# First projection rows of a two-layer decoder kernel: columns for shift and scale, sigmoid by the exponential, new planner costs

## The chip, the cores and the metric

The program runs on one core of one Trainium2 chip. The metric is the device time of one execution in microseconds; the median of three runs of the kernel before is 709.39 us. A core has five engines that run their own instruction streams and meet through semaphores: PE (TensorE, the matrix multiplier), DVE (VectorE), ACT (ScalarE), POOL (GpSimd) and SP (SyncE, which here only issues the DMA transfers). 16 DMA engines move data between HBM and SBUF.

## The reference, cut to what matters

Two layers over x of 256 rows and 1024 columns, all in float32. Each layer first makes six vectors of 1024 from the conditioning vector c, and uses two of them, shift and scale, on the normalized rows before its projections:

```python
cond = jax.nn.silu(c)                                  # c * sigmoid(c), 1024 numbers
for l in range(DEPTH):
    mod = (cond @ w_mod[l] + b_mod[l])[:, None, :]     # w_mod[l]: 1024 x 6144
    sh_a, sc_a, g_a, sh_f, sc_f, g_f = jnp.split(mod, N_MOD, axis=-1)
    h = rms_norm(x, norm_mix[l]) * (1 + sc_a) + sh_a
    proj = h @ w_in[l]                                 # 1024 x 3072: mq mk mv dq dk dv
    ...
    x = x + g_a * (jnp.concatenate([o_m, o_d], axis=-1) @ w_out[l])
    h = rms_norm(x, norm_ffn[l]) * (1 + sc_f) + sh_f
    x = x + g_f * ((jax.nn.silu(h @ w_gate[l]) * (h @ w_up[l])) @ w_down[l])
```

The weights are read once from HBM, some 157 MB. Only for layer 0 is nothing computed yet when its shift and scale are needed; for everything later they can be prepared beside other work.

## The kernel before, in words

**Products.** Every large product is made of float32 operands split in two parts, hi and lo, that TensorE multiplies at its faster float32 rate: `mm3` (L466 to L478) issues three matmuls of 128 x 512, hi*hi (L473), lo*hi (L474) and hi*lo (L475). There are 784 such triples in a fixed chain, in the order of the program text; the kernel's progress can be counted in them. `split` makes the two parts of a weight tile: ACT copies (`hi`, L463), DVE subtracts (`lo`, L464). Other matmuls (attention, transposes, the modulation) are plain float32.

**A planner sets the order.** The kernel text doesn't emit instructions but records them (`op`), and a list scheduler (`Plan.schedule`) puts them in order per engine, from a cost of each operation, latencies between engines (`DRAIN`, `WAKE`, `DMA_DONE`), the cost of a DMA (`c_dma`) and a rank for each group of operations (the table `RANK`, `TUNE`). Its times are used for the order alone. At run time each engine goes through its list strictly in that order and waits where an operand isn't there. All DMAs stand in one list on SP. Buffers are few: 3 of 1 MiB (`raw`), 2 of 512 KiB (`rawm`), 8 pairs of `hi` and `lo`, 12 of 256 KiB (`w`), 8 banks of PSUM (`ps`); a transfer waits until its buffer's last reader is done.

**The start of layer 0** (`start_layer0`) is the part that the change rewrites. It loads x, takes 1/rms of its rows (`x_rstd`, L552 squares on ACT), and goes through five blocks of output columns, of 1, 1, 2, 2 and 2 times 128 (`blocks`). For each block it needs the shift and the scale of these columns. w_mod comes in pieces in which partition p holds rows 8p to 8p+7, so that one block is eight terms (t = 0..7), each a 128-row product with one column of `cs` (silu(c)). The first `npe[b]` terms are matmuls (L923) of a stationary tile `cb`, in which each `cs` column is repeated 128 times, with w_mod as the moving operand: the result is the row, repeated on all partitions. The other terms are accumulated on DVE (`acc`, L926) and summed over partitions by one more matmul with ones (L928). Then: the scale row plus one times the gain row (L933, the gain loaded to all partitions), the shift row copied (L935, ACT), for both row tiles of x the scaling (L938) and the shift (L941), transposes on PE (L943), and the split of the transposed result into `hThi` (L949, ACT) and `hTlo` (L951, DVE). With these, and with the split rows of w_in for the same columns k, PE runs 6 triples for each of the 8 k (dq, dk and dv for two row tiles): 48 triples, after which the dq, dk and dv of layer 0 are complete.

```python
op(ACT, 1400.0, lambda: S.activation(cs.tile, cs.tile, AF.Silu), [cs], [cs])
```

This line (L448) makes silu(c) with a table of ACT that has to be loaded for it, and again a load for the tables used later (L449).

**Beside this** DVE accumulates the other sections of w_mod for the two layers (`mod_section`, L513: 80 instructions of 128 x 1024).

Of the kernel before, what the change touches and what calls it, by code (L numbers as in the profile page):

```python
# [52 lines left out]
class Op:  # L53
    __slots__ = ("eng", "cost", "fn", "deps", "succ", "left", "bufs", "tail", "boost", "idx", "ready", "end", "start", "soft", "main", "group")


class Plan:
# [1136 lines left out]
```

## Time and profile before

| | us |
|---|---|
| median of 3 runs | 709.39 |
| lowest, highest | 708.60, 710.76 |
| the profiled execution | 709.06 |
| its span, from the first to the last instruction | 706.9 |
| PE busy in the span | 666.8 (94%) |
| DVE busy | 528.5 (75%) |
| ACT busy | 391.2 (55%) |
| DMA queue of the loads, share of the 16 engines | 65.4% |

Times inside the trace are counted from the first instruction. A float32 matmul that isn't a transpose stands in the trace as two records, so L923 with 13 instructions has 26. Matmul records overlap, since they are pipelined: what one costs in a row of many is the distance from one start to the next, not its duration. The order of an engine's list tells what stands behind what, and only the trace tells how long.

### The profile page before, as it was taken

To read this page: it belongs to the slowest core of one execution; us is meant where nothing else is said; L and a number is where in the kernel's file an instruction comes from. 1 tells how busy PE (TensorE), PEld (TensorE's weight loads), DVE (VectorE), ACT (ScalarE), POOL (GpSimd) and SP (SyncE) were. 2 spreads that over 40 slices of the span, in tenths; PEclk is the share of its full clock that TensorE was granted. 3 is DMA by queue.
4 is the path that set the end of the run, shared out by engine and by line. 5 is a ranking of instruction groups with operands and counts; after the bars stand their busy time and mean duration, and the time that the engine had idled before them with its cause. 6 is when DMAs were issued, how large, how long until landed. Compare 5 with 4: busy or idle time off the path is not lost.

```text
span 706.9 us, 8834 instructions
## 1 busy us (share of the span) xinstructions
PE 666.8 (94%) x3085; PEld 520.7 (74%) x3085; DVE 528.5 (75%) x846; ACT 391.2 (55%) x836; POOL 17.0 (2%) x37
## 2 busy tenths in 40 slices
PE   2988999997999999999989999999999999999997
PEld 1656767775778887878768886788788888888885
DVE  3979899999886778787778998996886554464433
ACT  5335899755454544453345766998755444544420
POOL 2000020000000000000000000000000000000000
PEclk9999999999899999999999999999999999999999
DMA  8988885656678679888883589453537555555501
GB/s 267 346 279 296 314 304 178 219 168 227 221 252 284 230 264 313 304 315 295 268 290 134 192 295 318 175 190 110 179 119 249 188 187 194 194 179 178 179 1 59
DMA packets 92496, 158.25 MB, mean 224 GB/s; under 512 B 6030, under 2 KB 62234, under 8 KB 92452
## 3 DMA queue, kind: packets, MB, share of 16 engines
q1 hardware_dynamic: 92452, 157.69, 65.4%
q8 instruction: 24, 0.39, 0.2%
q14 instruction: 20, 0.16, 0.1%
HBM read 156.62 MB, written 1.05 MB: 223 GB/s over the span
## 4 chain that ended last, share of the span: by engine, by line
PE 56%; DMA 14%; issue 12%; DVE 11%; ACT 4%; SPq 1%; POOL 1%; DVEq 0%; ACTq 0%; POOLq 0%
PE ps L475 16%; PE ps L473 16%; PE ps L474 16%; DMA rawm<-in_w_mod_dram 7%; DVE acc L513 4%; DVE lo L464 3%; DMA raw<-in_w_mod_dram 3%; DMA raw<-in_w_in_dram 2%; ACT hi L463 2%; PE ps L674 2%; PE ps L923 1%; PE ps L735 1%; PE ps L1079 1%; ACT w L609 1%; DMA raw<-in_w_down_dram 1%
## 5 line engine op out<-in xcount | busy, mean ns | idle before, releaser
L464 DVE TENSOR_TENSOR lo<-raw,hi 128x1024 fp32r<-128x1024 f32 (+1 forms) x192 | 230.6, 1210 | 99.7 <-ACT hi L463 99.2
L463 ACT ACTIVATE hi<-raw 128x1024 fp32r<-128x1024 f32 (+1 forms) x192 | 198.9, 1050 | 170.8 <-PE ps L475 119.1
L473 PE MATMUL ps<-hi,hThi 128*128 128x512 f32 x544 | 224.0, 412 | 1.9 <-ACT w L609 1.3
L475 PE MATMUL ps<-hi,hTlo 128*128 128x512 f32 x544 | 216.8, 398 | 0.0
L474 PE MATMUL ps<-lo,hThi 128*128 128x512 f32 x544 | 216.5, 398 | 0.0
L473 PEld LDWEIGHTS ps<-hi,hThi 128*128 128x128 f32 x544 | 103.5, 190 | 27.2 <-issue 1.4
L475 PEld LDWEIGHTS ps<-hi,hTlo 128*128 128x128 f32 x544 | 103.0, 189 | 25.6 <-DVE hTlo L951 0.7
L474 PEld LDWEIGHTS ps<-lo,hThi 128*128 128x128 f32 x544 | 103.5, 190 | 24.9 <-issue 1.4
L513 DVE SCALAR_TENSOR_TENSOR acc<-rawm,cs,acc 128x1024 f32<-128x1024 f32 x80 | 102.5, 1281 | 21.5 <-DMA rawm<-in_w_mod_dram 18.7
L473 PE MATMUL ps<-hi,oThi 128*128 128x512 f32 x240 | 96.7, 403 | 3.1 <-ACT oThi L1086 2.3
L474 PE MATMUL ps<-lo,oThi 128*128 128x512 f32 x240 | 95.7, 399 | 1.6 <-DVE lo L464 1.6
L475 PE MATMUL ps<-hi,oTlo 128*128 128x512 f32 x240 | 95.8, 399 | 1.0 <-DVE oTlo L1088 0.8
L473 PEld LDWEIGHTS ps<-hi,oThi 128*128 128x128 f32 x240 | 45.4, 189 | 13.9 <-ACT oThi L1086 2.8
L474 PEld LDWEIGHTS ps<-lo,oThi 128*128 128x128 f32 x240 | 45.4, 189 | 13.4 <-DVE lo L464 3.2
L475 PEld LDWEIGHTS ps<-hi,oTlo 128*128 128x128 f32 x240 | 45.3, 189 | 12.7 <-DVE oTlo L1088 1.2
L692 ACT ACTIVATE w<-ps,sm,sm 128x128 f32<-128x128 f32 (+1 forms) x64 | 32.6, 530 | 7.0 <-DVE sm L687 7.0
L1077 ACT ACTIVATE w<-ps 128x256 f32<-128x256 f32 x44 | 16.7, 382 | 24.0 <-PE ps L475 23.8
L923 PE MATMUL ps<-raw,w 128*128 128x512 f32 (+1 forms) x26 | 14.4, 690 | 14.8 <-DMA raw<-in_w_mod_dram 14.8
L1078 DVE TENSOR_TENSOR w<-w,ps 128x256 f32<-128x256 f32 x44 | 18.1, 416 | 6.1 <-ACT w L1077 6.1
L552 ACT ACTIVATE w<-xs 128x512 f32<-128x512 f32 x16 | 10.0, 627 | 20.9 <-DVE xs L782 19.1
L926 DVE SCALAR_TENSOR_TENSOR acc<-raw,cs,acc 128x512 f32<-128x512 f32 (+1 forms) x27 | 17.0, 630 | 5.6 <-ACT hi L463 4.1
L1086 ACT ACTIVATE oThi<-ps 128x512 fp32r<-128x512 f32 x22 | 12.5, 592 | 15.1 <-PE ps L1079 15.1
(138 smaller groups left out, 593.1 us busy)
## 6 DMA issues: line engine op xcount, KB each, us to landing
rawm<-in_w_mod_dram SPq DMA_DIRECT2D x80, 512.0 KB
raw<-in_w_gate_dram SPq DMA_DIRECT2D x44, 512.0 KB
raw<-in_w_up_dram SPq DMA_DIRECT2D x44, 512.0 KB
raw<-in_w_down_dram SPq DMA_DIRECT2D x22, 1024.0 KB
raw<-in_w_in_dram SPq DMA_DIRECT2D x18, 1024.0 KB
raw<-in_w_mod_dram SPq DMA_DIRECT2D x32, 256.0 KB
raw<-in_w_out_dram SPq DMA_DIRECT2D x8, 1024.0 KB
raw<-in_w_in_dram SPq DMA_DIRECT2D x4, 768.0 KB
```

Of the source, the lines that this page charges most:

```text
L463: op(ACT, c_act(n, False), lambda: S.activation(hi[:, :n], raw[:, sl], AF.Copy), [raw], [hi], boost=boost)
L464: op(DVE, c_tt(n), lambda: V.tensor_tensor(lo[:, :n], raw[:, sl], hi[:, :n].bitcast(F32), op=ALU.subtract), [raw, hi], [lo], boost=boost)
L473: TE.matmul(ps[:, :], hi[:, k, tt], w[0][:, sl], start=start, stop=False)
L474: TE.matmul(ps[:, :], hi[:, k, tt], w[1][:, sl], start=False, stop=False)
L475: TE.matmul(ps[:, :], lo[:, k, tt], w[0][:, sl], start=False, stop=stop)
L513: op(DVE, c_stt(D), lambda raw=raw, t=t: V.scalar_tensor_tensor(acc[:, :], raw[:, :], cs[:, t : t + 1], acc[:, :], op0=ALU.mult, op1=ALU.a ...
L674: TE.matmul(pss[par][:, c], q, k, start=True, stop=False)
L692: op(ACT, c_act(n, True, 3), lambda ps=ps, pr=pr, j=j, c=c: S.activation(pr[:, j * n : (j + 1) * n], ps[:, j * n : (j + 1) * n], AF.Exp, b ...
L923: op(PE, 4 * W2 / 2.4 + 4.0, lambda r=r, t=t, ps=ps, W2=W2: TE.matmul(ps[:, :W2], cb[:, t * P : (t + 1) * P], r(), start=t == 0, stop=Fals ...
L926: op(DVE, c_stt(W2), lambda r=r, t=t, av=av: V.scalar_tensor_tensor(av(), r(), cs[:, t : t + 1], av(), op0=ALU.mult, op1=ALU.add), rk + [c ...
L1077: last_silu = op(ACT, c_act(FC), lambda: S.activation(sil[:, :FC], ps[:, :FC], AF.Silu), [ps], [sil], after=silu_set, boost=B)
L1078: op(DVE, c_tt(FC), lambda: V.tensor_tensor(sil[:, :FC], sil[:, :FC], ps[:, FC:], op=ALU.mult), [sil, ps], [sil], boost=B)
```

## The change

It has four parts.

1. `cs` is made as c / (1 + exp(-c)): one exponential on ACT from the table set that stays loaded, three small DVE instructions. The Silu line goes, and with it two of the table loads at the head.
2. The shift and scale of layer 0 are made as columns: w_mod is now the stationary operand and one column of `cs` the moving one, so that an L952 matmul has a moving operand of one column, and its result is a column with one number for each partition. There are 2*kw such matmuls for each term t in place of one wide one; `npe` rises from (3, 1, 4, 2, 3) to (6, 4, 4, 4, 4), which makes 68 of them, and 16 (L963) for the sums over partitions. DVE accumulates 18 terms in place of 27, and the first of a block is a plain product (L957), so that `acc` needs neither zeroing nor the bias row.
3. x is normalized and transposed before the modulation (L920, L922, L924), 16 transposes as before. Then the modulation of a 128-column slice is one DVE instruction with two per-partition numbers (L977), ACT copies `hThi` (L980), DVE subtracts `hTlo` (L982). The bias and gain come as three small loads of 8 x 128, transposed once (L912); the broadcast loads of the gain for layer 0 and the copies to `cb` go. While the first loads are under way, PE multiplies `ident` by `ones` 20 times (L900); the result is not used.
4. The planner's constants change (a switch between kinds of matmul costs 4 instead of 85, a DMA's latency is 280 longer, small DVE operations are cheaper, loads are slower), and with them all numbers of `RANK`; so the order of every engine changes over the whole program. The chain of 784 triples is the same.

```diff
-    SWITCH = 85.0
-    DMA_ISSUE, DMA_SETUP = 475.0, 650.0
-    DMA_DONE = {ACT: 910.0, DVE: 1000.0, POOL: 1000.0, PE: 1180.0, SP: 1000.0}
+    SWITCH = 4.0
+    DMA_ISSUE, POOL_ISSUE, DMA_SETUP = 475.0, 1000.0, 650.0
+    DMA_DONE = {ACT: 1190.0, DVE: 1280.0, POOL: 1280.0, PE: 1460.0, SP: 1280.0}
...
 def c_sm(n):
-    return 108.0 + 1.042 * n
+    return 70.0 + 1.042 * n
...
-    gate=8891.847, blocks=(1, 1, 2, 2, 2), npe=(3, 1, 4, 2, 3), early=(3.88, 5.44), late=(5.32, 1.29),
+    gate=8891.847, blocks=(1, 1, 2, 2, 2), npe=(6, 4, 4, 4, 4), early=(3.88, 5.44), late=(5.32, 1.29),
...
-    "start": (1678,),
+    "start": (3816,),
...
-    op(ACT, 1400.0, lambda: S.activation(cs.tile, cs.tile, AF.Silu), [cs], [cs])
-    act_set = [op(ACT, 1300.0, lambda: S.preload_act_table_set("natural_log_exp_and_others"), [cs], [])]
+    act_set = [op(ACT, 1300.0, lambda: S.preload_act_table_set("natural_log_exp_and_others"), [], [], boost=1e6)]
+    sg = fix("sg", [P, KT])
+    op(ACT, 110.0, lambda: S.activation(sg.tile, cs.tile, AF.Exp, scale=-1.0), [cs], [sg], after=act_set, boost=1e5)
+    op(DVE, c_sm(8), lambda: V.tensor_scalar(sg.tile, sg.tile, 1.0, None, op0=ALU.add), [sg], [sg], boost=1e5)
+    op(DVE, 120.0, lambda: V.reciprocal(sg.tile, sg.tile), [sg], [sg], boost=1e5)
+    op(DVE, c_sm(8), lambda: V.tensor_tensor(cs.tile, cs.tile, sg.tile, op=ALU.mult), [cs, sg], [cs], boost=1e5)
...
+        warm = buf("ps")
+        for _ in range(TUNE["warm"]):
+            op(PE, 214.0, lambda: TE.matmul(warm[:, :P], ident.tile, ones.tile, start=True, stop=True), [], [warm], boost=-1e6)
...
-        rstd = [x_rstd(t, B) for t in range(NT)]
+        for t in range(NT):
+            rstd = x_rstd(t, B)
+            for g in range(2):
+                h, pst = buf("w"), buf("ps")
+                op(DVE, c_ts(512), lambda h=h, t=t, g=g, rstd=rstd: V.tensor_scalar(
+                    h[:, :], xs[:, t, g * 512 : (g + 1) * 512], rstd[:, 0:1], None, op0=ALU.mult), [(xs, (t, g)), rstd], [h], boost=B)
+                op(PE, 4 * 109.0, lambda h=h, pst=pst: [TE.transpose(
+                    pst[:, k * P : (k + 1) * P], h[:, k * P : (k + 1) * P], ident.tile) for k in range(4)], [h], [pst], boost=B)
...
-                        op(PE, 4 * W2 / 2.4 + 4.0, lambda r=r, t=t, ps=ps, W2=W2: TE.matmul(
-                            ps[:, :W2], cb[:, t * P : (t + 1) * P], r(), start=t == 0, stop=False), [cb] + rk, [ps], boost=TUNE["smod"])
+                        op(PE, 2 * kw * TUNE["mv"], lambda r=r, t=t, ps=ps, kw=kw: [TE.matmul(
+                            ps[:, c : c + 1], r()[:, c * P : (c + 1) * P], cs[:, t : t + 1], start=t == 0 and c == 0, stop=False,
+                            skip_group_check=True)
+                            for c in range(2 * kw)], [cs] + rk, [ps], boost=TUNE["smod"])
...
+            for k in range(k0, k0 + kw):
...
-                op(DVE, c_stt(BW), lambda h=h, t=t, ra=ra, cols=cols, BW=BW: V.scalar_tensor_tensor(
-                    h[:, :BW], xs[:, t, cols], rstd[t][:, 0:1], ra[:, :BW], op0=ALU.mult, op1=ALU.mult),
...
-                op(DVE, c_tt(BW), lambda h=h, rs=rs, BW=BW: V.tensor_tensor(h[:, :BW], h[:, :BW], rs[:, :BW], op=ALU.add),
...
+                op(DVE, c_ts(SEQ), lambda h=h, k=k: V.tensor_scalar(
+                    h[:, :SEQ], xT(k), ash[:, 1, k : k + 1], ash[:, 0, k : k + 1], op0=ALU.mult, op1=ALU.add),
+                   [(ash, b)] + [(xrow(k), q) for q in keys], [h], boost=B)
+                op(ACT, c_act(SEQ, False), lambda h=h, k=k: S.activation(hThi[:, k], h[:, :SEQ], AF.Copy),
+                   [h], [(hThi, q) for q in keys], boost=B)
+                op(DVE, c_tt(SEQ), lambda h=h, k=k: V.tensor_tensor(hTlo[:, k], h[:, :SEQ], hThi[:, k].bitcast(F32), op=ALU.subtract),
+                   [h] + [(hThi, q) for q in keys], [(hTlo, q) for q in keys], boost=B)
```

**PE's list at the head of the program, up to the first triple of dq.** `raw` holds w_mod, `w_95` is `cb`. Before:

```order
L923 MATMUL ps_134<-raw_61,w_95 128x256 x3
L928 MATMUL ps_134<-acc_82,ones 128x256
L923 MATMUL ps_135<-raw_62,w_95 128x256
L943 MATMUL ps_136<-ident,w_89 128x128
L943 MATMUL ps_136<-ident,w_90 128x128
L923 MATMUL ps_137<-raw_63,w_95 128x512 x2
L473 MATMUL ps_138<-hi_66,hThi 128x512
```

And after, where `w_88` holds bias and gain, and `w_94`, `w_95`, `w_99`, `w_90` the normalized x:

```order
L900 MATMUL ps_134<-ones,ident 128x128 x20
L912 MATMUL ps_140<-ident,w_88 128x24
L922 MATMUL ps_136<-ident,w_94 128x128 x4
L922 MATMUL ps_137<-ident,w_95 128x128 x4
L952 MATMUL ps_138<-cs,raw_61 128x1 x2
L922 MATMUL ps_139<-ident,w_99 128x128 x4
L922 MATMUL ps_140<-ident,w_90 128x128 x4
L952 MATMUL ps_138<-cs,raw_61 128x1 x10
L963 MATMUL ps_138<-ones,acc_83 128x1 x2
L952 MATMUL ps_141<-cs,raw_62 128x1 x8
L483 MATMUL ps_134<-hi_66,hThi 128x512
```

The transposes have moved ahead of the block's modulation, and twelve one-column matmuls, two sums and the eight of a later block stand before the first triple.

**SP's list of transfers, from the weights of k = 5 to those of k = 7 before.** The `128x1536` are the dq, dk and dv rows of w_in for one k, the `128x4x512` are the next projection's (mq), `128x2x256` are shift and scale:

```order
L445 DMA raw_61<-in_w_in_dram 128x1536
L445 DMA raw_62<-in_w_mod_dram 128x2x256 x4
L445 DMA raw_63<-in_w_in_dram 128x1536
L445 DMA grope<-in_moba_q_norm_dram 128x2x16
L445 DMA grope<-in_moba_k_norm_dram 128x2x16
L445 DMA rawm_64<-in_w_mod_dram 128x1024
L445 DMA rawm_65<-in_w_mod_dram 128x1024
L445 DMA raw_61<-in_w_mod_dram 128x2x256 x4
L445 DMA raw_62<-in_w_in_dram 128x1536
L445 DMA raw_63<-in_w_in_dram 128x4x512
```

The same list after, from the end of the last block's w_mod to the weights of k = 7:

```order
L449 DMA rawm_64<-in_w_mod_dram 128x1024
L449 DMA raw_61<-in_w_mod_dram 128x2x256
L449 DMA rawm_65<-in_w_mod_dram 128x1024
L449 DMA raw_63<-in_w_in_dram 128x1536
L449 DMA grope<-in_moba_q_norm_dram 128x2x16
L449 DMA grope<-in_moba_k_norm_dram 128x2x16
L449 DMA raw_61<-in_w_in_dram 128x4x512
L449 DMA w_97<-in_diff_q_norm_dram 2x48
L449 DMA raw_62<-in_w_in_dram 128x4x512
L449 DMA acc_83<-in_b_mod_dram 1x1024
L449 DMA raw_63<-in_w_in_dram 128x1536
```

Both 1 MiB loads of mq now stand ahead of the weights of k = 7, and all of w_mod for the five blocks ahead of those of k = 6.

**DVE's list around the first block's modulation.** Before:

```order
L933 SCALAR_TENSOR_TENSOR w_98<-ps_134,w_92 128x128
L938 SCALAR_TENSOR_TENSOR w_89<-xs,sm_110,w_98 128x128
L938 SCALAR_TENSOR_TENSOR w_90<-xs,sm_111,w_98 128x128
L941 TENSOR_TENSOR w_89<-w_89,w_99 128x128
L941 TENSOR_TENSOR w_90<-w_90,w_99 128x128
L926 SCALAR_TENSOR_TENSOR acc_82<-raw_62,cs,acc_82 128x256 x2
L951 TENSOR_TENSOR hTlo<-ps_136,hThi 128x256
```

After:

```order
L969 TENSOR_TENSOR ash<-ps_138,mcol 128x2
L972 TENSOR_TENSOR ash<-ash,mcol 128x1
L977 TENSOR_SCALAR w_91<-rowA,ash 128x256
L474 TENSOR_TENSOR lo_79<-rawm_64,hi_71 128x1024
L982 TENSOR_TENSOR hTlo<-w_91,hThi 128x256
```

Five instructions on rows have become three, two of them on one or two numbers per partition; the transposes no longer stand between them.

## Rows read from the trace of the kernel before

**Rows 1.** Windows by stage: length, busy us of each engine (instructions), granted clock, DMA.

```profile
core 0: us, PE busy (x) PEld busy (x) DVE busy (x) ACT busy (x) POOL busy (x), PEclk, DMA share, GB/s
0.00:22.30 22.30, 8.42 (x16) 4.57 (x17) 10.05 (x30) 11.58 (x23) 4.37 (x23) 1.00 0.93 287
22.30:75.10 52.80, 48.08 (x183) 33.73 (x182) 46.87 (x105) 24.39 (x50) 1.91 (x2) 0.97 0.88 297
...
130.00:178.30 48.30, 41.31 (x224) 31.35 (x224) 45.03 (x77) 28.70 (x58) 1.91 (x2) 0.99 0.70 234
178.30:203.40 25.10, 24.08 (x99) 19.26 (x99) 21.21 (x30) 14.17 (x21) 0.00 (x0) 0.88 0.58 195
```

**Rows 2.** Windows, the third matmul of each triple (L475) on PE alone.

```profile
22.35:75.12 52.77, 19.59 (x48) 0.97 0.88 296
```

**Rows 3.** Timeline of PE at the head: start, length, what, idle before it.

```profile
19.59 3.75 PE L923 MATMUL ps<-raw,w 128*128 128x512 f32 x4 [1.15 <-DMA raw<-in_w_mod_dram]
22.36 1.42 PE L473 MATMUL ps<-hi,hThi 128*128 128x512 f32 x1
```

**Rows 4.** Timeline of ACT at the head.

```profile
8.18 0.21 ACT L448 ACTIVATE cs<-cs 128x8 f32<-128x8 f32 x1
```

**Rows 5.** The chain that ended last, its pieces up to 80 us: start, length, what.

```profile
6.58 6.47 DMA raw<-in_w_mod_dram
...
14.03 5.43 DMA raw<-in_w_mod_dram
...
60.59 0.87 PE ps L928 x2
...
65.15 0.48 DVE hTlo L951
...
71.60 7.92 DMA raw<-in_w_in_dram
```

**Rows 6.** The chain again, at 476 us: plain float32 matmuls, then a triple.

```profile
475.51 0.44 PE ps L762 x4
475.95 1.73 PE ps L735 x16
...
479.68 0.23 PE ps L474
```

**Rows 7.** Groups of the whole trace by form: count, busy us, mean ns, idle before.

```profile
L464 DVE TENSOR_TENSOR lo<-raw,hi 128x1024 fp32r<-128x1024 f32 x188 | 228.0, 1221 | 99.7 <-ACT hi L463 99.2
...
L463 ACT ACTIVATE hi<-raw 128x1024 fp32r<-128x1024 f32 x188 | 196.8, 1059 | 168.3 <-PE ps L475 119.1 <-DMA raw<-in_w_in_dram 17.6 <-DMA raw<-in_w_up_dram 15.8
...
L735 PE MATMUL ps<-v,w 128*128 128x64 f32 x96 | 12.0, 273 | 0.7 <-ACT w L729 0.7
...
L735 PE MATMUL ps<-v,w 128*128 128x128 f32 x48 | 6.1, 278 | 0.0
...
L713 DVE TENSOR_SCALAR w<-w,sm 128x256 f32<-128x256 f32 x4 | 1.2, 350 | 0.0
...
L713 DVE TENSOR_SCALAR w<-w,sm 128x128 f32<-128x128 f32 x4 | 0.9, 282 | 0.0
```

**Rows 8.** Groups of DVE by line in the first 68 us.

```profile
L938 DVE SCALAR_TENSOR_TENSOR w<-xs,sm,w 128x256 f32<-128x256 f32 (+1 forms) x10 | 3.9, 429 | 0.2
L941 DVE TENSOR_TENSOR w<-w,w 128x256 f32<-128x256 f32 (+1 forms) x10 | 3.2, 364 | 0.0
L951 DVE TENSOR_TENSOR hTlo<-ps,hThi 128x512 fp32r<-128x512 f32 (+1 forms) x5 | 2.9, 579 | 0.3 <-ACT hThi L949 0.2
...
L933 DVE SCALAR_TENSOR_TENSOR w<-ps,w 128x256 f32<-128x256 f32 (+1 forms) x5 | 1.8, 369 | 1.6 <-PE ps L928 1.6
```

**Rows 9.** The same groups of DVE, different shapes kept apart.

```profile
L926 DVE SCALAR_TENSOR_TENSOR acc<-raw,cs,acc 128x512 f32<-128x512 f32 x15 | 11.2, 748 | 0.5 <-DMA raw<-in_w_mod_dram 0.3
...
L926 DVE SCALAR_TENSOR_TENSOR acc<-raw,cs,acc 128x256 f32<-128x256 f32 x12 | 5.8, 483 | 5.1 <-ACT hi L463 4.1 <-DMA raw<-in_w_mod_dram 0.8
...
L951 DVE TENSOR_TENSOR hTlo<-ps,hThi 128x256 fp32r<-128x256 f32 x2 | 0.8, 425 | 0.3 <-ACT hThi L949 0.2
```

More of the change, by code (lines that the diff above doesn't have):

```diff
@@ L53 @@
 class Op:
-    __slots__ = ("eng", "cost", "fn", "deps", "succ", "left", "bufs", "tail", "boost", "idx", "ready", "end", "start", "soft", "main", "group")
+    __slots__ = ("eng", "cost", "fn", "deps", "succ", "left", "bufs", "tail", "boost", "idx", "ready", "end", "start", "soft", "main", "group", "dma")
 class Plan:
@@ L95, in lat, with op @@
         return self.DRAIN[a.eng] + self.WAKE[b.eng]
-    def op(self, eng, cost, fn, r=(), w=(), after=(), boost=0.0, main=False, rel=0.0):
+    def op(self, eng, cost, fn, r=(), w=(), after=(), boost=0.0, main=False, rel=0.0, dma=False):
         o = Op()
+        o.dma = dma or eng == SP
         o.eng, o.cost, o.fn, o.boost, o.idx = eng, cost, fn, boost + self.rank, len(self.ops)
@@ new lines @@
+    "rinv": (-1500, 2371, -208, 950, 1164, 289, -2963, -9126,),
+    "mix": (1523, 3197, 2768, 4844, 1594, -16,),
+    "pv": (6765, 3568, 8042, 1461, 4973, 2747, 17442, 7474, 7107, 3467, 1991, -177, 8585, -196, 4, 1600, 369,
+        2091,),
+    "heads": (1383, -142, 308, 92, 9069, 2506, -52, -98,),
+    "res": (2238, 41, 501, 208, -2541, -1369, -65, 340, -214, -306, 3383, 44, -3105, -12087, -1831, 7215,),
+    "xrstd": (-108, 0, 6334, 2075, 3602, -745,),
+    "norm": (1681, 571, 313, -858, 2199, 1254, -136, 7, 9104, 27, -787, -1009,),
@@ new lines, in start_layer0 @@
+        for i, src in enumerate((b_mod[0, SH_A * D : (SH_A + 1) * D], b_mod[0, SC_A * D : (SC_A + 1) * D], norm_mix[0])):
+            dma(lambda i=i: mrow[i * KT : (i + 1) * KT, :P], src.rearrange("(k p) -> k p", p=P), 4096, [(mrow, i)])
+        op(PE, 60.0, lambda: TE.transpose(pst[:, : 3 * KT], mrow[: 3 * KT, :P], ident[: 3 * KT, : 3 * KT]), [mrow], [pst], boost=B)
+        op(ACT, 120.0, lambda: S.activation(mcol.tile, pst[:, : 3 * KT], AF.Copy), [pst], [mcol], boost=B)
+        op(DVE, c_sm(8), lambda: V.tensor_scalar(mcol[:, KT : 2 * KT], mcol[:, KT : 2 * KT], 1.0, None, op0=ALU.add),
+           [mcol], [mcol], boost=B)
@@ new lines, in start_layer0 @@
+        for t in range(NT):
[6 more added lines that the diff above has]
+                    pst[:, k * P : (k + 1) * P], h[:, k * P : (k + 1) * P], ident.tile) for k in range(4)], [h], [pst], boost=B)
+                op(ACT, c_act(512), lambda pst=pst, t=t, g=g: S.activation(
+                    v3(xrow(4 * g)[:, :], SEQ)[:, :, t * P : (t + 1) * P], v3(pst[:, :], P), AF.Copy),
+                   [pst], [(xrow(4 * g), (k, t)) for k in range(4 * g, 4 * g + 4)], boost=B)
@@ L927, in start_layer0 @@
                             av(), r(), cs[:, t : t + 1], av(), op0=ALU.mult, op1=ALU.add), rk + [cs, (a, b)], [(a, b)], boost=TUNE["smod"])
-            op(PE, 4 * W2 / 2.4 + 4.0, lambda ps=ps, av=av, W2=W2, npe=npe: TE.matmul(
-                ps[:, :W2], ones.tile, av(), start=not npe, stop=True), [(a, b)], [ps], boost=B)
-            plan.mark("shead")
-            gn = gain_row(0, SC_A, cols)
-            ra, rs, pst = buf("w"), buf("w"), buf("ps")
-            op(DVE, c_stt(BW), lambda ra=ra, ps=ps, gn=gn, BW=BW, W2=W2: V.scalar_tensor_tensor(
-                ra[:, :BW], ps[:, BW:W2], 1.0, gn[:, :BW], op0=ALU.add, op1=ALU.mult), [ps, gn], [ra], boost=B)
@@ L946, in start_layer0 @@
-            keys = [(k, t) for t in range(NT) for k in range(k0, k0 + kw)]
-            dst = lambda q, k0=k0, kw=kw: q[:, k0 : k0 + kw]
-            src = lambda pst=pst, kw=kw: v3(pst[:, : kw * SEQ], SEQ)
-            op(ACT, c_act(W2), lambda src=src, dst=dst: S.activation(dst(hThi), src(), AF.Copy),
-               [pst], [(hThi, k) for k in keys], boost=B)
-            op(DVE, c_tt(W2), lambda src=src, dst=dst: V.tensor_tensor(dst(hTlo), src(), dst(hThi).bitcast(F32), op=ALU.subtract),
-               [pst] + [(hThi, k) for k in keys], [(hTlo, k) for k in keys], boost=B)
+            if npe < KT:
+                op(PE, 2 * kw * TUNE["mv"], lambda ps=ps, av=av, kw=kw, npe=npe: [TE.matmul(
+                    ps[:, c : c + 1], av()[:, c * P : (c + 1) * P], ones[:, 0:1], start=not npe and c == 0, stop=True,
+                    skip_group_check=True)
+                    for c in range(2 * kw)], [(a, b)], [ps], boost=B)
@@ new lines, in start_layer0 @@
+            for k in range(k0, k0 + kw):
+                h = buf("w")
+                keys = [(k, t) for t in range(NT)]
+                op(DVE, c_ts(SEQ), lambda h=h, k=k: V.tensor_scalar(
[5 more added lines that the diff above has]
+                   [h] + [(hThi, q) for q in keys], [(hTlo, q) for q in keys], boost=B)
```

94 lines of the change are left out of this document (44 added, 50 removed), and 47 rows, old and new, of the table RANK.

## The prediction

> **What bounds the kernel now.** I read first the windows by stage [rows 1], then a progress count [rows 2], then the head's timelines [rows 3, 4], then the chain [rows 5]. In the windows the reader is to see that PE is nearly always busy from 22 us on, and where it isn't: nothing useful happens on it in the first 22.3 us, and 7.0 of the 48.3 us from 130 to 178.3 are idle, while DVE has 45.0 of them. The count says how far the kernel is: 48 third matmuls of triples, all of dq, dk and dv, are through at 75.1 us. From there to the end of the span at 706.9 are 631.8 us, which the change leaves the same work. So the question is at what time the 48th triple ends after the change, and whether the rest keeps its length.
>
> Two lines run through the start. One is **the transfers**. The chain shows w_mod landing at 13.05 and at 19.46 [rows 5]; by the list of transfers 2.63 and 4.63 MiB had then been asked for, which is 0.312 MiB per us. Drawn on, the line gives 80.3 us for the 23.6 MiB up to the last load of layer 0's mv; the chain has it at 71.60 + 7.92 = 79.5. The transfers thus ran without a hole for 80 us (DMA share 0.93 and 0.88 [rows 1]), so the change gets no byte earlier than this line except by moving it up the list. The other is **PE's own work**: the first triple starts at 22.36 [rows 3], and 52.8 us hold 33.6 us of triples (144 matmuls of 0.233, as in [rows 6]), the wide modulation matmuls, and waits.
>
> **Part 1, the sigmoid.** cs was there at 8.39 [rows 4], early, since w_mod landed only at 11.36 [rows 3]. After the change its load stands behind 2.26 MiB, which is 11.9 us by the line, and the exponential stands on ACT behind two copies hi (1.06 and some 0.6 [rows 7]) and two copies of transposed x. I take 12.7 for its end and three small DVE instructions with hand-overs: cs at 13.5. The block's w_mod is complete at 13.5 too (2.77 MiB), so the later cs costs nothing by itself, and the two table loads saved are worth nothing either.
>
> **Part 2, columns.** No row has a moving operand of one column. The nearest is L735, plain float32 with 64 moving columns: its records are 1.73/16 = 0.108 us apart [rows 6], 64 and 128 columns have the same mean of 273 and 278 ns [rows 7], and a transpose costs 0.44/4 = 0.11 [rows 6]. So with few columns the price has stopped falling, and an instruction of two records costs 0.22. The other end is 0.43: two records each as long as one of 512 columns at full speed, 0.87/2 [rows 5], if nothing overlaps; below 0.11 for a record no row goes. I take 0.22, since L735 has the same form of stationary operand. Of the 84 matmuls 22 stand ahead of the first triple, 62 among the triples: 62 x 0.22 = 13.6.
>
> The Trainium skill, "TensorE: Matmul & The Clock Gate", section "Back-to-back issue gap", lets a matmul of 1 to 64 columns go down to a floor of about 62 ns when the sequencer decodes it. Two records would then be 0.12, and the 62 matmuls 7.7 us; no row here goes below 0.108 per record.
>
> **DVE.** Removed: 27 accumulations, 11.2 + 5.8 = 17.0 [rows 9], and the modulation of five blocks, 3.9 + 3.2 + 2.9 + 1.8 = 11.8 [rows 8]. Added: 13 accumulations, 9 x 0.748 + 4 x 0.483 = 8.7 [rows 9]; 5 products with one number per partition, 0.35 each with 256 columns [rows 7], and with the 0.53 ns per column between 282 and 350, 0.49 with 512: 2.2; for x, 4 x 0.49 = 2.0; 8 slices at 0.35 and 8 differences at 0.42 [rows 7, 9]: 6.2; some 14 tiny ones of 0.16: 2.2. That is 21.3 against 28.8: 7.5 us less on an engine that has 46.9 of 52.8 us there.
>
> **The path of a block.** From the sums to the finished hTlo it took 65.15 + 0.48 - 60.59 = 5.0 [rows 5]. The transposes and three of five wide DVE instructions leave it; 0.16 + 0.16 + 0.35 + 0.4 + 0.42 and five hand-overs of 0.2 are 2.5.
>
> **Part 3, the head of PE.** The 20 warm-up matmuls start at 1.6 and end by 10.3 even at half speed (0.43 each); only ACT's copy of the columns waits for them, and x isn't there sooner. Then: 12 matmuls, 8 transposes of the second row tile and 2 sums, 14 x 0.22 + 8 x 0.11 = 4.0 from 13.6, to 17.6. In PE's list 8 matmuls of the third block stand next; their w_mod lands at 18.3 (4.27 MiB), so they end at 20.1, which is also when the first hT is ready (17.6 + 2.5). **First triple at 20.1** instead of 22.4.
>
> From there PE has 33.6 + 13.6 + 0.5 (four transposes of q) = 47.7 us, and waits: 1.4 for the third block's second half (6.27 MiB, 24.7 us; PE is there at 23.3), 0.6 for its sums, 0.3 at k = 7. **48th triple at 70.1.** The transfers' line agrees: 18.1 MiB up to the weights of k = 7 land at 62.6, the split takes 1.06 + 1.22 and hand-overs [rows 7], then 18 matmuls of 0.233 are 4.2: 69.4. That two MiB of mq now stand ahead of k = 7 costs 6.4 us on this line, and gives them back, as the next 24 matmuls of mq find their weights there. 75.1 - 70.1 = **5.0 us gained**.
>
> **Part 4, the new order.** The chain of triples is the same, and transposes, scores and sums lie between the same triples or a few further. Every wait after 75 us is dealt anew, though. From 130 to 178.3 DVE is 93% busy and PE loses 7.0 us. Of DVE's 7.5 us, 5.0 go into the shift; the other 2.5 can come off this wait. I take **2.0**. For the rest I take nothing: PE's idle time there is small and a new order can move it either way, by 4 us as I guess from the 8.0 idle us of 130 to 203.4 [rows 1], half of them.
>
> **The sum.** The profiled execution took 709.06, 2.2 more than its span and 0.3 below the median of the runs, so it stands for them. 709.06 - 5.0 - 2.0 = 702.1; I say **702**.
>
> **Rivals.** *More:* DVE's whole saving comes off at 130 to 178.3, and the half-speed stretch after it shrinks: the granted clock of 0.88 over 25.1 us [rows 1] is 6 us at 1.2 GHz, 3.0 us lost. 702.1 - 0.5 - 3.0 and another 1 of the 7.0: 697.5. For it, DVE's share of 93%; against it, that the same work stands ahead of the norm at 178. Chance 0.15.
>
> *Half speed at the head.* In the first 23 us of before PE ran at 1.2 GHz: four records of 512 columns took 3.75, 0.86 from start to start, against 0.43 later [rows 3, 5], though the clock's column says 1.00; it rose only after 19.59, when PE worked without a hole. After the warm-up PE has only transposes and then nothing until 13.6. If it falls back, 22 matmuls and 8 transposes cost twice: 22 x 0.22 + 0.9 = 5.7, of which 2.1 vanish in the waits for transfers: 705.7. For it, the hole of some 4 us; against it, that the stretch from 22.3 to 75.1 us has 4.7 idle us and kept 0.97 of the clock [rows 1]. Chance 0.12. The Trainium skill, "TensorE: Matmul & The Clock Gate", section "Part 4: PE-mode transpose", says that transposes don't count as PE work for the clock gate, which speaks for this rival; no row of before shows it.
>
> *Given back:* the start gains 5, the new order adds waits of the size of those at 130 to 203.4, 8.0 x 0.6 = 5 in place of the 2.0 gained: 709. For it, that all ranks are new; against it, that PE has little idle time left to be moved. Chance 0.13.
>
> *Slower:* a one-column matmul costs 0.43, a whole w_mod tile being loaded for one column. 62 x 0.21 = 13 us more on PE, which bounds the start: 715. It decides from the price at which 7 us are gone, 7/62 = 0.11 more, 0.33 each. Against it stand the equal means of 64 and 128 columns. Chance 0.08. That the change doesn't do what it says (the sigmoid no earlier) is in the forecast already.
>
> **How the numbers follow.** Forecast 0.52, more 0.15, half speed 0.12, given back 0.13, slower 0.08. A run of this kernel can tell 0.3% from no change, 2.1 us. Faster than 706.9: forecast, more and half speed, 0.79, less a tail of 0.01: 0.78. Within: given back, 0.13. Slower: 0.09. The forecast's own range is 698 to 706 (transfers up to 2 us late, the 4 us of the new order). The range for 8 in 10 runs from 693, the more-rival with the new order's luck, to 711, given back with its bad luck; it leaves out the slower case.
>
> **What the changed profile would show.** Right: first triple near 20, 48 third matmuls of triples by 70, records of the one-column matmuls some 0.11 apart, the weights of k = 7 landed near 62.6, PE idle less than 7 us in the stage of the first output projection. Wrong: one-column records 0.2 apart or more; PE waiting at k = 6 or 7 for transfers after 64; the 48th triple after 73; or an early 48th triple with more idle time behind it than the 21.5 us of before (40.1 of the span, less 13.9 and 4.7 up to 75.1 us [rows 1]), which would mean that the new order decides and not the start.

## The result and the profile after

The changed kernel takes 700.8 us in the median of four runs, beside 710.1 for the kernel before: a ratio of 0.988, with a 95% interval of 0.984 to 0.992. Forecast were 702 us, and faster by more than 0.3%. One of the four runs of wide64 below, of 697.4 us, is over 1.5% above the fastest; it counts as a slow one and is left out of the median and the ratio. The number held, and most of its working did not, so that it held by luck: the start, from which 5.0 of the 7.0 us were to come, became 9.5 us longer, and the rest of the program, from which 2.0 were expected, 18.1 us shorter.

Counted in triples, whose matmuls are called the main ones below, the first starts at 22.72 us (before 22.36; forecast 20.1) and the 48th ends at 84.58 (before 75.11; forecast 70.1). The windows up to there and behind it, which answer to [rows 1]:

```profile
core 0: us, PE busy (x) PEld busy (x) DVE busy (x) ACT busy (x) POOL busy (x), PEclk, DMA share, GB/s
0.00:84.60 84.60, 79.21 (x374) 69.42 (x375) 51.85 (x131) 33.55 (x80) 3.81 (x22) 0.80 0.78 260
...
20.00:68.00 48.00, 48.00 (x217) 42.04 (x216) 27.77 (x77) 11.52 (x18) 0.00 (x0) 0.71 0.68 229
...
84.60:698.30 613.70, 602.22 (x2885) 478.67 (x2884) 469.16 (x711) 357.56 (x759) 10.47 (x12) 1.00 0.65 221
```

From 20 to 68 us PE isn't idle for a moment, and yet the granted clock is 0.71: for over half of that time TensorE was at 1.2 GHz. The transfers' share is 0.68 there; in the same order with the clock up it is 0.82 and 0.90 (wide64 and wide64fill below). The same stretch behind the start in the kernel before, a new row of it:

```profile
core 0: us, PE busy (x) PEld busy (x) DVE busy (x) ACT busy (x) POOL busy (x), PEclk, DMA share, GB/s
75.10:706.90 631.80, 610.30 (x2890) 482.38 (x2889) 471.58 (x713) 355.20 (x765) 10.75 (x12) 0.99 0.63 216
```

The work of PE is the same but for a few records. 10.0 of the 18.1 us are idle time of PE (21.5 to 11.5), the other 8.1 are busy time. By the granted clock 13.1 us of this stretch were at 1.2 GHz before and 3.7 after, which is 4.7 of the 8.1; the last 3.4 were not traced.

PE's timeline at the head shows where the start lost its time (start, length, what, records; in brackets the idle time before it). It answers to [rows 3]:

```profile
1.46 7.46 PE L900 MATMUL ps<-ones,ident 128*128 128x128 f32 x40 [1.46 <-POOL eps_t L445]
...
12.82 0.61 PE L952 MATMUL ps<-cs,raw 128*128 128x1 f32 x4 [2.19 <-DVE cs L457]
13.29 1.25 PE L922 MATMUL ps<-ident,w 128*128 128x128 f32 x8
14.32 4.27 PE L952 MATMUL ps<-cs,raw 128*128 128x1 f32 x20
...
25.43 6.82 PE L952 MATMUL ps<-cs,raw 128*128 128x1 f32 x32
...
42.95 0.40 PE L485 MATMUL ps<-hi,hTlo 128*128 128x512 f32 x1
...
45.28 4.18 PE L952 MATMUL ps<-cs,raw 128*128 128x1 f32 x32
49.33 0.78 PE L483 MATMUL ps<-hi,hThi 128*128 128x512 f32 x1
49.90 0.63 PE L484 MATMUL ps<-lo,hThi 128*128 128x512 f32 x1
50.33 0.63 PE L485 MATMUL ps<-hi,hTlo 128*128 128x512 f32 x1
...
59.09 2.82 PE L952 MATMUL ps<-cs,raw 128*128 128x1 f32 x24
61.77 0.73 PE L483 MATMUL ps<-hi,hThi 128*128 128x512 f32 x1
```

At 14.32 twenty one-column records take 4.27 us, 0.21 each, twice the forecast 0.11. At 59.09 twenty-four take 2.82, or 0.12 each: that is the price at full clock, and the forecast's. The row at 45.28 is the telling one. The main matmuls ahead of it (0.40 long, 0.23 from start to start) run at 2.4 GHz, nothing waits between, and behind these 32 records the next ones stand 0.43 apart: the clock fell while PE worked through one-column matmuls. It came back only after 13 more matmuls.

### The profile page after: what moved, and what is told of

The parts are those of the page before. It is cut to its first block, busy times and chain, and to the rows that moved or that the text cites. A ratio compares the mean times of both kernels' runs of the same rounds, so it can differ in the third digit from the quotient of the medians.

```text
span 698.3 us, 9171 instructions
## 1 busy us (share of the span) xinstructions
PE 681.4 (98%) x3258; PEld 548.1 (78%) x3258; DVE 521.0 (75%) x841; ACT 391.1 (56%) x837; POOL 14.3 (2%) x34
## 4 chain that ended last, share of the span: by engine, by line
PE 78%; DVE 13%; DMA 5%; ACT 2%; issue 1%; POOL 0%; DVEq 0%; ACTq 0%; POOLq 0%
PE ps L483 22%; PE ps L484 22%; PE ps L485 21%; DVE acc L523 3%; DVE lo L474 3%; PE ps L952 3%; DMA rawm<-in_w_mod_dram 3%; DMA raw<-in_w_in_dram 2%; PE ps L684 1%; PE ps L745 1%; PE ps L1110 1%; PE ps L900 1%; DVE w L789 1%; DVE xs L792 1%; PE ps L645 1%
## 5 line engine op out<-in xcount | busy, mean ns | idle before, releaser
L483 PE MATMUL ps<-hi,hThi 128*128 128x512 f32 x544 | 223.3, 410 | 1.6 <-ACT w L619 1.6
L484 PE MATMUL ps<-lo,hThi 128*128 128x512 f32 x544 | 218.9, 402 | 1.4 <-DVE lo L474 1.4
L485 PE MATMUL ps<-hi,hTlo 128*128 128x512 f32 x544 | 217.2, 399 | 0.0
L485 PEld LDWEIGHTS ps<-hi,hTlo 128*128 128x128 f32 x544 | 104.1, 191 | 25.3
L483 PEld LDWEIGHTS ps<-hi,hThi 128*128 128x128 f32 x544 | 104.3, 192 | 24.8 <-ACT w L619 1.7
L483 PE MATMUL ps<-hi,oThi 128*128 128x512 f32 x240 | 97.2, 405 | 0.8 <-ACT oThi L776 0.8
L485 PE MATMUL ps<-hi,oTlo 128*128 128x512 f32 x240 | 94.9, 395 | 0.3 <-DVE oTlo L778 0.3
L485 PEld LDWEIGHTS ps<-hi,oTlo 128*128 128x128 f32 x240 | 45.1, 188 | 11.6 <-DVE oTlo L778 0.7
L483 PEld LDWEIGHTS ps<-hi,oThi 128*128 128x128 f32 x240 | 45.1, 188 | 10.7 <-ACT oThi L776 1.0
L952 PEld LDWEIGHTS ps<-cs,raw 128*128 128x128 f32 x136 | 23.6, 268 | 2.8 <-DVE cs L457 2.4
L952 PE MATMUL ps<-cs,raw 128*128 128x1 f32 x136 | 23.2, 302 | 2.2 <-DVE cs L457 2.2
L980 ACT ACTIVATE hThi<-w 128x256 fp32r<-128x256 f32 x8 | 3.0, 416 | 36.0 <-DVE w L977 36.0
L684 PE MATMUL ps<-qkT,qkT 64*128 64x128 f32 (+1 forms) x128 | 19.8, 375 | 0.2 <-DVE rowA L540 0.2
```

The lines of the kernel that those rows point to most:

```text
L483: TE.matmul(ps[:, :], hi[:, k, tt], w[0][:, sl], start=start, stop=False)
L484: TE.matmul(ps[:, :], hi[:, k, tt], w[1][:, sl], start=False, stop=False)
L485: TE.matmul(ps[:, :], lo[:, k, tt], w[0][:, sl], start=False, stop=stop)
L684: TE.matmul(pss[par][:, c], q, k, start=True, stop=False)
L952: op(PE, 2 * kw * TUNE["mv"], lambda r=r, t=t, ps=ps, kw=kw: [TE.matmul(ps[:, c : c + 1], r()[:, c * P : (c + 1) * P], cs[:, t : t + 1], s ...
```

## The experiments

The times are medians; each ratio is to the kernel before on the same chip, with its 95% interval. "48th" is the end of the 48th triple, "rest" what follows up to the end of the span, both in the profiled execution, which can lie 4 us off the median. Line numbers are each kernel's own: L952 of the changed kernel is L955 or L958 where lines were added, its triples (L483 to L485) L486 to L488.

| kernel | us | ratio | 48th | rest |
|---|---|---|---|---|
| before | 709 to 711 | 1 | 75.1 | 631.8 |
| after | 700.8 | 0.988 (0.984 to 0.992) | 84.6 | 613.7 |
| nowarm | 702.9 | 0.988 (0.982 to 0.993) | 85.2 | 617.3 |
| fill | 700.5 | 0.985 (0.978 to 0.992) | 82.8 | 617.5 |
| wide64 | 691.2 | 0.972 (0.966 to 0.979) | 75.0 | 614.4 |
| wide64fill | 689.3 | 0.974 (0.968 to 0.979) | 71.1 | 615.0 |
| wide64fill3 | 688.7 | 0.973 (0.967 to 0.978) | 70.6 | 619.9 |
| before_sig | 709.4 | 1.001 (0.998 to 1.005) | 74.2 | 635.3 |
| before_newplan | 753.2 | 1.061 (1.056 to 1.066) | 80.0 | 669.2 |
| after_oldplan | 745.9 | 1.050 (1.044 to 1.055) | 84.1 | 655.6 |
| oldstart_newrest | 708.6 | 1.000 (0.997 to 1.003) | 72.0 | 634.3 |
| newstart_oldrest | 736.4 | 1.041 (1.035 to 1.047) | 85.7 | 647.3 |
| wide64fill_oldrest | 721.6 | 1.019 (1.013 to 1.024) | 70.8 | 648.5 |

### The clock at the start: wide64, wide64fill, wide64fill3, fill, nowarm

**wide64** gives the modulation's matmuls 64 equal columns, at the same number of records and in the same order, with one copy on DVE added (the sums and the reading of their result are changed likewise, not shown):

```diff
+    csw = rowgf.tile
+    cs_mult = plan.ops[-1].fn
+    plan.ops[-1].fn = lambda: [cs_mult(), V.tensor_copy(v3(csw[:, : KT * 64], 64), bc(cs[:, :], 64))]
...
-    ps[:, c : c + 1], r()[:, c * P : (c + 1) * P], cs[:, t : t + 1], start=t == 0 and c == 0, stop=False,
+    ps[:, c * 64 : (c + 1) * 64], r()[:, c * P : (c + 1) * P], csw[:, t * 64 : (t + 1) * 64], start=t == 0 and c == 0, stop=False,
```

> The changed kernel with 64 moving columns in place of one: each column of cs is repeated 64 times (one copy on DVE of 128x512 ahead of the first L952), L952 and L963 multiply by 64 equal columns, and the result is read from every 64th column of PSUM. Order, number of matmuls and everything else stay. Theory A, the one-column matmuls let the clock fall: the granted clock from 20 to 68 us rises from 0.71 to over 0.95, the matmuls cost 0.22 each (0.11 a record), the 48th triple ends at 70 to 75 us in place of 84.6, and the time is 688 to 697, depending on how much of the gain the waits behind the start take. Theory B, the clock fell for another reason (the idle stretch of 2.2 us before cs is ready, or the start's waits): clock 0.70 to 0.75 there, 48th triple at 84 to 86, time 700 to 703.

The 48th triple ends at 74.97, 9.6 us earlier, and the time falls by some 10 us: theory A. The window of 20 to 68 us, to be read against the one above:

```profile
core 0: us, PE busy (x) PEld busy (x) DVE busy (x) ACT busy (x) POOL busy (x), PEclk, DMA share, GB/s
20.00:68.00 48.00, 48.00 (x268) 41.91 (x269) 36.15 (x95) 17.70 (x26) 0.95 (x1) 0.94 0.82 275
```

PE has the same 48.00 busy us and gets through 51 records more. The clock is 0.94, just short of the expected 0.95, because the head is still slow until 26 us. Its timeline, and three windows of it:

```profile
12.58 1.11 PE L955 MATMUL ps<-rowgf,raw 128*128 128x64 f32 x4 [2.66 <-DVE rowgf L460]
...
15.19 4.37 PE L955 MATMUL ps<-rowgf,raw 128*128 128x64 f32 x20
...
26.27 3.68 PE L955 MATMUL ps<-rowgf,raw 128*128 128x64 f32 x32
```

```profile
9.70:12.50 2.80, 0.22 (x3) 0.00 (x0) 2.55 (x9) 1.72 (x6) 0.00 (x0) 1.00 1.08 347
12.60:23.50 10.90, 10.90 (x52) 10.90 (x52) 7.43 (x15) 4.43 (x7) 0.00 (x0) 0.50 1.10 342
26.30:30.20 3.90, 3.90 (x37) 3.90 (x36) 0.00 (x0) 0.00 (x0) 0.00 (x0) 1.00 0.29 67
```

0.22 a record at 15 us, 0.115 at 26 us. So there are two causes: within the start the single columns, and at the head something else. The clock was up until PE had waited for cs, and down from 12.6 us on; and 10.9 us of transposes and matmuls of 64 columns without a hole did not bring it back. It rose behind the first six main matmuls.

**wide64fill** puts five unused matmuls of 128x512 behind the transposes of the first row tile, where PE waited 2.66 us:

```diff
+                if (t, g) == (0, 1):
+                    last_tr = plan.ops[-1]
+                    last_tr.fn = lambda f=last_tr.fn: [f()] + [TE.matmul(warm[:, :512], ident.tile, xs[:, 0, :512], start=True, stop=True) for _ in range(5)]
```

> The changed kernel with 64 moving columns (as in wide64), and beside that five unused matmuls of 128x512 on PE behind the transposes of the first row tile, where PE waited 2.66 us for cs in wide64. Theory A, the half speed at the head comes from that stretch without matmuls: with it filled the first L955-kind records are 0.11 apart from 12.6 us on in place of 0.21, the first triple starts at 19 to 22 us in place of 23.8, the 48th triple ends 1 to 4 us earlier than the 74.97 of wide64, time 688 to 692. Theory B, the clock falls at the head for another reason (the transposes, or the matmuls of few columns themselves): the records stay 0.21 apart until 25 us, first triple at 24 to 26, time 692 to 696.

Theory A. The timeline, and a window of the unused matmuls:

```profile
9.76 4.46 PE L929 MATMUL ps<-xs,ident 128*128 128x512 f32 x10
14.06 0.55 PE L958 MATMUL ps<-rowgf,raw 128*128 128x64 f32 x4
14.45 1.04 PE L925 MATMUL ps<-ident,w 128*128 128x128 f32 x8
15.33 2.34 PE L958 MATMUL ps<-rowgf,raw 128*128 128x64 f32 x20
...
20.31 0.50 PE L486 MATMUL ps<-hi,hThi 128*128 128x512 f32 x1 [0.41 <-ACT hThi L986]
```

```profile
9.80:14.00 4.20, 4.20 (x12) 1.87 (x11) 4.03 (x12) 1.63 (x5) 0.00 (x0) 1.00 1.08 367
```

Twenty records now take 2.34 us, 0.117 each; the first triple starts at 20.31 (forecast for the change: 20.1) and the 48th ends at 71.1 (forecast 70.1). From 20 to 68 us the clock is 1.00 and the transfers' share 0.90. The unused work ran at 2.4 GHz throughout, 0.43 a record, which is what a record of 512 plain float32 columns takes at full clock (0.87/2, [rows 5]). It lasted longer than the 2.66 us that it filled, so that the first columns start at 14.06 in place of 12.58, and it still paid. **wide64fill3** has three of them in place of five:

> As wide64fill with three unused matmuls of 128x512 in place of five, since the five ended 1.5 us after cs was ready. If three hold the clock: the first L955-kind matmul at 12.6 us with records 0.11 apart, first triple 0 to 1 us earlier than 20.3, time 687 to 689.5. If not: records 0.21 apart up to 25 us as in wide64, time 691 to 694.

The clock held and the first triple started at 19.81. By their times the three wide versions can't be told apart; by their intervals all three beat the changed kernel, by 10 to 12 us of median, and they are the fastest of the study. What the filled head adds to them, 3.9 us at the 48th triple, is read from the profile alone.

**fill** has the five matmuls, but single columns:

> The changed kernel with one moving column as it is, and the five unused matmuls of 128x512 behind the transposes of the first row tile (as in wide64fill, without the 64 columns). Theory A, the one-column matmuls alone make the clock fall: the run of them at 14 to 20 us begins at 0.11 to 0.12 a record and goes to 0.21 within it, the matmuls of 25 to 45 us are as slow as in the changed kernel, 48th triple at 81 to 85 us, time 697 to 703. Theory B, the idle stretch at the head is the main cause: records 0.11 to 0.13 apart throughout the first 45 us, 48th triple at 74 to 80 us, time 690 to 696.

Theory A in the time and in the 48th triple. Its timeline:

```profile
15.33 2.29 PE L955 MATMUL ps<-cs,raw 128*128 128x1 f32 x20
17.48 0.58 PE L966 MATMUL ps<-ones,acc 128*128 128x1 f32 x4
17.93 2.21 PE L955 MATMUL ps<-cs,raw 128*128 128x1 f32 x16
20.32 0.80 PE L483 MATMUL ps<-hi,hThi 128*128 128x512 f32 x1 [0.18 <-ACT hThi L983]
...
23.20 6.82 PE L955 MATMUL ps<-cs,raw 128*128 128x1 f32 x32
```

The columns begin at 2.29/20 = 0.115 and are at 6.82/32 = 0.21 eight us later, with no idle time worth the name between. In wide64fill the same place keeps its clock. That settles the main cause: not the wait at the head, the single columns.

**nowarm** takes the warm-up's 20 matmuls out:

> The changed kernel without the 20 warm-up matmuls (L900); order and everything else stay. Theory A, the warm-up's effect on the clock is lost before the triples begin, since the one-column matmuls run at half speed anyway: first triple at 23.5 and 48th triple at 84.6, each within 0.5 us, time within 2 us of 700.8. Theory B, the warm-up saves the transposes and the first columns from half speed: first triple 1 to 2 us later, time 702 to 704.

```profile
19.51 3.55 PE L952 MATMUL ps<-cs,raw 128*128 128x1 f32 x16
```

0.22 a record, as with the warm-up. The first triple starts 0.2 us and the 48th ends 0.6 us later than in the changed kernel, the time is 2.1 us longer, at the edge of both theories and within the spread of the runs (the ratio to the kernel before is 0.988 in both). So the warm-up as it stands is worth at most a little: its clock is lost before the triples.

### The sigmoid: before_sig

> The kernel before with part 1 alone: cs by the exponential and three small DVE instructions, at the place of the Silu, and one table load less; order of everything else as before. Theory A, worth nothing, since w_mod lands after cs is ready in either case: first triple at 22.4 and 48th at 75.1, each within 0.3 us, time within 2 us of 709.5. Theory B, ACT's head is on the way of 1/rms and with 1.3 us less the first block is ready earlier: 48th triple 0.5 to 1.3 us earlier, time 708 to 709.

No difference in time (1.001, interval 0.998 to 1.005), which is theory A. In the profiled execution the 48th triple ends 0.9 us earlier, as theory B had it, and the rest is 3.5 us longer; in the times, which spread over 7 us, neither can be seen. cs is ready at 8.95 us, and the first accumulation on DVE waits for w_mod until 11.50 in any case. (A second load of the table, at 6.80, stayed in this kernel; that it would count elsewhere was not tried.)

### The order: four mixtures

**before_newplan** and **after_oldplan** exchange the planner's constants and all of RANK:

> The kernel before with the planner's constants and the whole table RANK of the changed kernel: part 4 alone; the start keeps its rows, its Silu and its npe. Theory A, the new order is what shortens the rest of the program: from the 48th triple to the end 610 to 620 us in place of 631.8, and with a 48th triple at 73 to 80 us a time of 686 to 701. Theory B, the rest is shorter because DVE has less to do at the start, or because the late start lets loads and splits get ahead: from the 48th triple to the end 628 to 636 us, time 704 to 714.

> The changed kernel with the planner's constants and the table RANK of the kernel before: parts 1 to 3 without part 4. Theory A, the new order shortens the rest and the new start costs time: 48th triple at 82 to 90 us, from there 628 to 636 us to the end, time 712 to 725. Theory B, the rest is shorter because of the new start: from the 48th triple to the end 612 to 620 us, time 698 to 708.

Neither theory gave this: both mixtures are some 40 us slower than the kernels they come from. In before_newplan PE waits twice for the sums of a section of w_mod that isn't loaded yet:

```profile
265.71 0.80 PE L527 MATMUL ps<-hi,onesr 128*128 128x512 f32 x1 [14.40 <-ACT hi L520]
287.40 0.80 PE L527 MATMUL ps<-hi,onesr 128*128 128x512 f32 x1 [17.64 <-ACT hi L520]
```

A rank is added to the length of the path behind an operation, so a table that gives a good order for one program and its constants need not give one for another; exchanging it measures nothing about the order that it gave.

So I kept the orders themselves. In **oldstart_newrest** and **newstart_oldrest** the planner runs as in the one kernel until the 48th triple is placed, and then takes each engine's operations in the recorded order of the other:

```diff
...
+            if mains == 48 and todo is None:
+                todo = {e: [o for o in sorted((o for o in self.ops if o.start is None and o.eng == e), key=lambda o: place[o.idx])] for e in now}
...
```

> The start of the kernel before (its rows, Silu, constants and ranks, up to the 48th triple), and from there on each engine's list in the order of the changed kernel; 46 of some 2600 operations stand elsewhere, where a buffer was not free. Theory A, the rest is shorter by its new order alone: 48th triple at 75 us as before, from there 612 to 618 us to the end in place of 631.8, time 690 to 697. Theory B, the rest is shorter because DVE or the loads stood better when it began: from the 48th triple to the end 625 to 635 us, time 702 to 713.

> The start of the changed kernel up to the 48th triple, and from there on each engine's list in the order of the kernel before; 50 of some 2600 operations stand elsewhere, where a buffer was not free. Theory A, the rest is shorter by its new order alone: 48th triple at 84 to 86 us, from there 628 to 636 us to the end, time 715 to 723. Theory B, the new start leaves DVE or the loads better placed: from the 48th triple to the end 612 to 622 us, time 699 to 709.

Taken whole, both miss: 634.3 and 647.3 us of rest, worse than either kernel with its own. (The 48th triple of oldstart_newrest ended at 72.0, where 75 was expected; why was not followed up.) But the rest falls into two parts. The windows of oldstart_newrest, split behind the 128th triple:

```profile
72.04:186.20 114.16, 96.69 (x507) 73.45 (x508) 94.02 (x204) 79.22 (x277) 4.80 (x7) 0.94 0.63 212
186.20:706.30 520.10, 511.94 (x2385) 409.41 (x2382) 377.22 (x514) 279.65 (x496) 4.77 (x5) 1.00 0.64 216
```

the changed kernel:

```profile
84.60:179.10 94.50, 90.52 (x501) 68.81 (x500) 90.94 (x197) 78.37 (x264) 5.69 (x7) 1.00 0.73 247
179.10:698.30 519.20, 511.70 (x2384) 409.86 (x2384) 378.22 (x515) 279.19 (x495) 4.78 (x5) 1.00 0.63 217
```

and the kernel before:

```profile
75.10:172.80 97.70, 91.03 (x502) 68.29 (x501) 89.64 (x192) 75.66 (x265) 5.01 (x6) 1.00 0.67 234
172.80:706.90 534.10, 519.27 (x2388) 414.08 (x2388) 381.94 (x522) 279.54 (x501) 5.74 (x6) 0.99 0.62 212
```

Behind the 128th triple the new order takes 520.1 us on the old start, 519.2 on the new one and 518.6 to 521.4 in wide64, wide64fill, wide64fill3, fill and nowarm; the old order takes 534.1 on its own start, 537.7 in before_sig, and 542.4 and 544.8 on the new start. So some 14 us or more belong to **the new order alone**, on either start. Up to the 128th triple an order needs its own start: 94.5 and 97.7 us with it, 114.2 with the other's. There PE waits in oldstart_newrest for attention's steps on DVE and ACT:

```profile
81.54 0.63 PE L722 MATMUL ps<-ident,w 128*128 128x128 f32 x4 [4.32 <-DVE w L721]
...
129.06 2.08 PE L822 MATMUL ps<-v,w 128*128 128x128 f32 x8 [4.89 <-ACT w L816]
...
142.06 2.05 PE L822 MATMUL ps<-v,w 128*128 128x128 f32 x16 [2.96 <-ACT w L816]
```

**wide64fill_oldrest** tests whether the old order fails on the new start only because that ends late:

> The start of wide64fill (48th triple at 71.1 us), and from the 48th triple on each engine's list in the order of the kernel before. Theory A, the old order's 647 us on the changed start came from the start ending 10 us later than the transfers: with the early start 628 to 636 us from the 48th triple to the end, time 701 to 709. Theory B, the old order doesn't fit what the new start has already done and left, whenever it ends: 642 to 652 us, time 715 to 725.

Theory B: 648.5 us with the 48th triple at 70.8, much as the 647.3 with 85.7. And with the new order the rest is 613.7 to 619.9 us in the six kernels that have the changed start, wherever that ends: it is 614.4 and 615.0 in wide64 and wide64fill, whose starts end 10 and 13 us earlier, and 613.7 in the changed kernel. The gain of the rest is thus not the late start's doing, and what the start gains reaches the end.

## Why the prediction was right, and where it wasn't

The parts of the program between two places of the triple chain, before and after, in us:

| triples | before | after | difference | forecast |
|---|---|---|---|---|
| up to the 48th | 75.11 | 84.58 | +9.5 | -5.0 |
| to the 96th | 53.54 | 52.48 | -1.1 | 0 |
| to the 160th | 77.94 | 67.98 | -10.0 | -2.0 |
| to the 256th | 69.89 | 71.52 | +1.6 | 0 |
| to the 384th | 101.45 | 93.16 | -8.3 | 0 |
| to the end of the span | 328.97 | 328.58 | -0.4 | 0 |

They sum up to -8.6 us of span, where -7.0 was forecast. Two large errors of opposite sign met: that the time came out 1.2 us from the forecast is luck.

**The price of a one-column matmul** was the term that failed. The step took it from rows at full clock and assumed that the clock stays up; the argument for that was a stretch with 4.7 idle us which kept 0.97 [rows 1]. But within the start it was not idle time that brought it down. At full clock the price is right (0.12 a record, 0.117 with 64 columns), at 1.2 GHz it is the 0.43 that the slower-rival named, for a reason that no rival had. By the distances of records from 12 to 85 us the start has 168 records of columns and sums at a mean of 0.157 us in the changed kernel and 0.109 in wide64fill, some 8 us; and 46 main matmuls in place of 14 are over 0.3 us from the next, some 7 us. That is the difference of 13.5 in the 48th triple, once 1.7 us are taken off, by which wide64fill's columns start later (14.06 against 12.82) and its waits are longer. The half-speed rival was right that the wait ahead of cs lets the clock fall, and about right on what the head loses by it: its 5.7 us, less 2.1, are 3.6, and wide64fill gains 3.9 over wide64. What it left out is the rest of the start, where the single columns brought the clock down twice more, at 48 and 62 us; and in the changed kernel itself the first four records behind the wait are still 0.12 apart (12.82 to 13.29), so that the fall came only behind them. Two of the prediction's own signs of being wrong came: records 0.2 apart, and a 48th triple after 73.

The Trainium skill, "TensorE: Matmul & The Clock Gate", section "Back-to-back issue gap", gives a floor of about 62 ns for small matmuls when the sequencer decodes them. No row of few columns in this case came near it: none took less than 0.108 us a record in the mean. Its section "Part 4: PE-mode transpose", by which transposes don't count as busy PE the same way, is neither borne out nor refuted: the transposes of the head stand beside the idle time, and wide64fill, where the clock held through eight of them, has matmuls on both sides.

**What held once the clock was up.** The first triple at 20.31 and the 48th at 71.1 in wide64fill, against 20.1 and 70.1; so the terms of the start were of the right size: the matmuls at 0.22, the transfers' line (the chain has the weights of k = 7 landing at 57.35 + 6.00 = 63.35, forecast 62.6) and the sum of the waits (1.9 us, forecast 2.3). But the waits stand elsewhere, at the first triple and at k = 7, in place of the third block, so this agreement is in part luck. The path of a block is 3.3 us in the changed kernel, from the sums at 18.45 to 21.76, in place of 2.5. The rows of DVE there:

```profile
19.48 0.16 DVE L969 TENSOR_TENSOR ash<-ps,mcol 128x2 f32<-128x2 f32 x1 [1.52 <-PE ps L963]
...
20.20 1.22 DVE L474 TENSOR_TENSOR lo<-rawm,hi 128x1024 fp32r<-128x1024 f32 x1
21.34 0.42 DVE L982 TENSOR_TENSOR hTlo<-w,hThi 128x256 fp32r<-128x256 f32 x1
```

The split of 1.22 us stands between L977 and hTlo in the order's rows ahead of the prediction too, and the sum left it out.

**The sigmoid** is worth nothing, as forecast: before_sig.

**The new order** was the mis-sized term. The 2.0 us had the right place, DVE's waits from 130 us on, but 10.0 came off there. The waits of 173 to 178 us went, and with them the half-speed stretch behind them [rows 1], which only the more-rival counted: of the 10.0 us 5.4 are idle time (8.5 to 3.1), and the clock went from 0.96 to 1.00. That DVE's smaller load did it is not shown: the old order on the new start takes 105.0 us up to the 128th triple, longer than the 97.7 on its own. The 8.3 us from the 256th to the 384th triple had no term at all. There the kernel before shows PE waiting, and running slow behind it:

```profile
363.44 0.50 PE L473 MATMUL ps<-hi,oThi 128*128 128x512 f32 x1 [2.33 <-ACT oThi L1086]
...
364.93 0.67 PE L475 MATMUL ps<-hi,oTlo 128*128 128x512 f32 x1 [0.75 <-DVE oTlo L1088]
```

```profile
276.48:377.93 101.45, 97.04 (x418) 76.87 (x417) 77.88 (x80) 42.23 (x56) 1.91 (x2) 0.98 0.85 296
```

and the changed one hardly at all:

```profile
276.56:369.72 93.16, 92.96 (x409) 74.81 (x409) 70.06 (x69) 41.21 (x51) 0.96 (x1) 1.00 0.84 288
```

4.2 of the 8.3 us are idle time, some 2 are the clock (0.98 of 101 us), and the stretch has 9 records of PE fewer, which stand elsewhere now. The prediction took "a new order can move it either way" as a reason for zero, and bounded it by the idle time of 130 to 203 us alone; 21.5 idle us behind the start, and the slow matmuls behind each wait, were there to be won.

**Open.** How many columns between 1 and 64 hold the clock was not tried. Which of the constants and ranks removed those waits was not tried apart. Nor is it settled what in the state that a start leaves makes the other's order 6 to 20 us worse up to the 128th triple.

## What to carry to other kernels

A price taken from rows holds only at the clock of those rows: before work is moved onto PE, ask what it does to the clock of the matmuls around it, and where columns are free, use them: here 64 cost what one did and kept the clock. A term that can go "either way" needs a size from the waits that stand in the trace, not a zero. And a tuned order belongs to its program; to test it alone, replay the order, not the numbers that made it.
